# RMS statistics summed in pairs, a halved last block, and pooled output slots in a two-layer convolution trunk on eight cores

## Chip, cores, metric

The kernel is one program for all eight cores of one Trainium2 chip. Each core takes one prompt of 2048 tokens and 16 of the 128 short sequences of 4 tokens, so every core has the same work on its own data: 2112 tokens, cut into four blocks of 512 and one of 64. The metric is device time in microseconds (us) of the slowest core.

The program has a second, slower state in some executions, whatever the kernel: the cores of a die show a lower granted clock (the share of its full clock that TensorE is given: 0.81 to 0.98 on the slow dies here, 0.98 to 0.99 elsewhere) and the time is 3 to 19 per cent longer.

## Reference, cut to what matters

```python
def rmsnorm(x, g):
    xf = x.astype(jnp.float32)
    xn = xf * lax.rsqrt(jnp.mean(xf * xf, axis=-1, keepdims=True) + RMS_EPS)
    return xn.astype(x.dtype) * g

def hybrid_layer(x, ...):                       # D_MODEL 1024, DEPTH 2
    h = rmsnorm(x, norm_g)
    p = h @ w_in                                # 7 * 1024 columns: a_val, a_gate, z_a, gb, gc, hb, z_b
    u = a_val * sigmoid(a_gate)
    y_a = silu(head_layernorm(causal_dwconv(u, width 31))) * silu(z_a)
    y_b = gb * causal_dwconv(gc * hb, width 3) * silu(z_b)
    return x + concat(y_a, y_b) @ w_out         # and the last convolution rows
# two layers, then rmsnorm(x, final_g)
```

So there are three norms: one ahead of layer 0 (at the start, while x is still being loaded), one between the layers ("the border"), and one at the end.

## The kernel before: the parts that matter

The kernel is not written in program order. Each operation is entered into a scheduler with the tiles it reads and writes and a modelled duration; a simulation of the engines in Python then fixes one static order for each engine and queue.

x is held feature-major (128 features by tokens, eight tiles `k`). A norm needs the sum of squares over features, that is over partitions, which a matmul with a constant 1/1024 matrix (`ones_s`) gives. ScalarE squares two tiles at once; TensorE takes one matmul for each tile, eight for a block:

```python
def rms_stat(q, fill=None):                       # q: token block
    b = V("bank", "stat")
    for kp in range(4):
        s = V("tmp")
        act(... Square of x tiles 2*kp and 2*kp+1 -> tmph[:, s.slot, 0:2*n] ...)
        mm("stat", b, n, [(ones_s, tmph[:, s.slot, i*n:(i+1)*n]) for i in range(2)], ...)
    # ScalarE: Ln, then Exp(-0.5 *) -> r

def rms_apply(gcol0, q, r, final=False):          # eight VectorE multiplies x * g * r
    ...                                           # final: the result goes out, two tiles a DMA

def out_final(l, chunks, yslots, order, gcol0, final):    # last output projection of a layer
    for q in order:                               # last layer: blocks [0, 1, 4, 2, 3]
        for m in range(KC):
            out_block(q, m, lhs, ws + tps, yslots)        # 8 matmuls, VectorE adds the bank to x
        r = rms_stat(q)
        rms_apply(gcol0, q, r, final)
```

The gate outputs y of a layer need eight full-width slots at the end, and there are only five. The other three are borrowed from `u_sb` (two) and `up_sb`, the convolution's buffers. A borrowed slot has the resource of the *whole* buffer, so a reader of block 0 waits for the writer of block 4:

```python
def y_res(slot, q):
    if slot < NY:        return [y_r[slot][q]]    # own slot: one resource for each block
    if slot < NY + 2:    return u_r[slot - NY]    # borrowed: all blocks
    return [up_r, uph_r]
```

The convolution of head group A goes by way of DRAM, all on the queue of the SP engine, in order: `scr_u <- u_sb` (768 KB), `up_sb <- scr_u` (regrouped), convolution and LayerNorm in tile `big`, `scr_c <- big` (640 KB), `big <- scr_c` (640 KB, "the conv row"). The projection z_A of the same head is entered with the conv row as an explicit dependency, although the matmul doesn't read it (a ScalarE operation does, whose result is multiplied with z_A later):

```python
    o = spdma(... big[:, cn.slot] <- scr_c[l, j] ...)
    cn_of[(l, j, "op")] = o
def ln_z(l, j, slot):
    ...
    bz = proj(w, q, after=[cn_of[(l, j, "op")]], name=f"z{j}.{q}")
```

## Time and profile before

| before | us |
|---|---|
| time, median of 3 runs | 1146.0 (1145.72, 1146.0, 1204.93) |
| spans of the eight cores in the profiled run | 1138.2 to 1143.9 |

First the page of the slowest core (core 4): span, busy time with share and number of instructions, and the head of the chain of waits, which follows the work that ended last back to what released it.

```profile
span 1143.9 us, 20833 instructions; the slowest of 8 cores (1138.2 to 1143.9 us)
...
PE 1111.0 (97%) x7118; PEld 547.9 (48%) x7118; DVE 758.1 (66%) x1547; ACT 431.9 (38%) x680; POOL 187.7 (16%) x336
...
PE 92%; DMA 4%; DVE 2%; issue 1%; ACT 1%; SPq 0%; DVEq 0%; POOL 0%; ACTq 0%; POOLq 0%
```

TensorE (PE) is busy 97% of the span and is 92% of the chain: the time can only fall if TensorE gets less work or fewer gaps. The list of TensorE's waits on the same core (what it waited for: us in all, times, the longest; `psb` is the matmul's output, `wsl` and `toep` hold weights, L550 is a line of the kernel) has few gaps:

```profile
PE psb L550 <- ACT tmp L571: 6.0, 8, 1.6
PE psb L550 <- DVE h_sb L590: 5.5, 2, 2.9
PE psb L550 <- DMA wsl<-w_in_r: 5.2, 4, 1.9
PE psb L550 <- DVE up_sb L791: 4.5, 2, 2.2
PE psb L844 <- DVE ones_s L848: 1.5, 1, 1.5
```

The first two are the norms of the start and the end (squares, then h). The fourth is the borrowed slot. In the timeline (start, duration, engine, line, operation, count, in brackets the idle time before and what ended it) it stands at the head of layer 0's last output projection:

```profile
516.16 1.86 PE L550 MATMUL psb<-y_sb,wsl 128*128 128x512 bf16 x4 [2.24 <-DVE up_sb L791]
517.82 0.63 PE L550 MATMUL psb<-y_sb,toep 128*128 128x512 bf16 x1
...
519.46 1.03 PE L550 MATMUL psb<-y_sb,wsl 128*128 128x512 bf16 x4
```

After the wait eight matmuls take 3.30 us, 0.41 us each on average (0.427 us from start to start in the middle of the stretch); then they start every 0.215 us. The granted clock was 0.52 in this stretch (516.16 to 519.50), and 1.00 from 57 to 514. So a wait can cost more than its own length.

The end, on the same core (rows of other engines and weight loads left out). The last output matmul starts at 1129.09 and the next matmul at 1129.30; then the squares, the ones-matmuls, Ln and Exp, eight multiplies and the output follow one another:

```profile
1129.30 1.03 PE L550 MATMUL psb<-tmp,ones_s 128*128 128x512 bf16 x4
1129.38 2.47 DVE L800 TENSOR_TENSOR x_sb<-x_sb,psb 128x512 f32<-128x512 f32 x4
...
1133.15 0.59 PE L550 MATMUL psb<-tmp,ones_s 128*128 128x512 bf16 x2 [0.60 <-ACT tmp L571]
...
1134.53 0.63 ACT L581 ACTIVATE tmp<-tmp 128x512 f32<-128x512 f32 x1
1135.26 5.39 DVE L590 SCALAR_TENSOR_TENSOR x_sb<-x_sb,vecs_sb,tmp 128x512 f32<-128x512 f32 x8 [3.40 <-ACT tmp L581]
```

### The profile page before, as it was taken

What the parts mean: (1) busy time and instruction counts of PE and PEld (TensorE: products, weight loads), DVE (VectorE), ACT (ScalarE), POOL (GpSimd) and SP (SyncE); (2) the same over time, 40 slices, a digit from 0 to 9 for tenths busy, and PEclk for the clock granted to TensorE, in tenths of its full rate; (3) what the DMA queues carried; (4) which work ended last, traced back from release to release, by engine and by line L of the source; (5) the groups of instructions that cost most, each with busy time, mean ns of one, the idle gap of its engine ahead of it and who ended that gap; (6) DMA issues with size and microseconds to landing.
All of it is one profiled execution on the core that took longest, in us unless ns stands there. A gap on an engine that the chain in (4) does not pass through costs nothing.

```text
span 1143.9 us, 20833 instructions; the slowest of 8 cores (1138.2 to 1143.9 us)
## 1 busy us (share of the span) xinstructions
PE 1111.0 (97%) x7118; PEld 547.9 (48%) x7118; DVE 758.1 (66%) x1547; ACT 431.9 (38%) x680; POOL 187.7 (16%) x336
## 2 busy tenths in 40 slices
PE   6899999999999999999999999999999999999995
PEld 4345454455445455444444455445544545544442
DVE  2674866986876587653674486598688566774475
ACT  3751443343413444533342143433451253454232
POOL 1421222022102021000032122111120202110000
PEclk8999999999999999999999999999999999999998
DMA  8837667466726466731021757656761745563043
GB/s 192 230 82 144 101 133 136 84 107 118 129 35 111 84 119 111 127 67 19 1 43 30 144 114 141 139 87 113 126 98 42 142 87 104 92 81 105 1 157 147
DMA packets 177286, 117.97 MB, mean 103 GB/s; under 512 B 139104, under 2 KB 150240, under 8 KB 177120
## 3 DMA queue, kind: packets, MB, share of 16 engines
q0 software_dynamic: 32544, 48.41, 28.9%
q1 hardware_dynamic: 144496, 68.21, 23.9%
q8 instruction: 59, 0.97, 0.3%
q14 instruction: 43, 0.35, 0.1%
q10 hardware_dynamic: 144, 0.03, 0.0%
HBM read 132.24 MB, written 36.19 MB: 147 GB/s over the span
## 4 chain that ended last, share of the span: by engine, by line
PE 92%; DMA 4%; DVE 2%; issue 1%; ACT 1%; SPq 0%; DVEq 0%; POOL 0%; ACTq 0%; POOLq 0%
PE psb L550 88%; DMA wsl<-w_in_r 2%; PE psb L666 2%; DMA x_sb<-x_d 2%; PE psb L668 2%; DVE x_sb L590 1%; DVE h_sb L590 0%; SPq L834 0%; DVE x_sb L800 0%; ACT tmp L571 0%; ACT tmp L581 0%; ACT tmp L579 0%; DVE up_sb L791 0%; ACT L579 0%; DVE tmp L789 0%
## 5 line engine op out<-in xcount | busy, mean ns | idle before, releaser
L550 PE MATMUL psb<-h_sb,wsl 128*128 128x512 bf16 (+1 forms) x4480 | 821.8, 343 | 10.8 <-DVE h_sb L590 5.5
L550 PEld LDWEIGHTS psb<-h_sb,wsl 128*128 128x128 bf16 x4480 | 373.2, 98 | 417.1 <-issue 16.6
L550 PE MATMUL psb<-y_sb,wsl 128*128 128x512 bf16 (+1 forms) x960 | 186.6, 343 | 4.5 <-DVE up_sb L791 4.5
L800 DVE TENSOR_TENSOR x_sb<-x_sb,psb 128x512 f32<-128x512 f32 (+1 forms) x240 | 133.8, 591 | 63.3 <-PE psb L550 62.6
L541 POOL DMA_DIRECT2D wsl<-w_in_r x112 | 60.3, 545 | 432.5 <-PE psb L550 321.4
L550 PEld LDWEIGHTS psb<-y_sb,wsl 128*128 128x128 bf16 x960 | 82.3, 98 | 94.6 <-issue 5.7
L782 DVE SCALAR_TENSOR_TENSOR tmp<-vbuf,cw_b_sb,tmp 128x512 f32<-128x512 bf16 (+1 forms) x160 | 102.8, 660 | 21.9 <-POOL vbuf L764 11.6
L607 DVE SCALAR_TENSOR_TENSOR u_sb<-tmp,psb 128x512 bf16<-128x512 f32 (+1 forms) x80 | 47.3, 592 | 98.6 <-PE psb L550 88.3
L605 ACT ACTIVATE tmp<-psb 128x512 f32<-128x512 f32 (+1 forms) x80 | 41.1, 521 | 144.5 <-PE psb L550 139.6
L752 DVE TENSOR_TENSOR vbuf<-psb,tmp 128x512 bf16<-128x512 f32 (+1 forms) x80 | 47.3, 594 | 63.8 <-PE psb L550 61.3
L644 DVE COPY toep<-wt_sb 32x512 bf16<-32x512 bf16 x256 | 77.4, 304 | 12.7 <-DMA wt_sb<-wt_d 0.9
L571 ACT ACTIVATE tmp<-x_sb 128x1024 bf16<-128x1024 f32 (+1 forms) x60 | 52.6, 901 | 82.7 <-DVE x_sb L800 75.3
L741 ACT ACTIVATE tmp<-psb 128x512 f32<-128x512 f32 (+1 forms) x80 | 40.6, 521 | 103.8 <-PE psb L550 92.6
L787 ACT ACTIVATE tmp<-psb 128x512 f32<-128x512 f32 (+1 forms) x80 | 41.2, 521 | 96.3 <-PE psb L550 89.9
L779 ACT ACTIVATE tmp<-vbuf,cw_b_sb 128x512 f32<-128x512 bf16 (+1 forms) x80 | 50.9, 642 | 57.0 <-DVE vbuf L752 51.6
L673 DVE TENSOR_TENSOR big<-psb,cbt_sb 128x320 bf16<-128x320 f32 x128 | 62.1, 485 | 14.6 <-PE psb L668 10.6
L750 ACT ACTIVATE tmp<-psb 128x512 f32<-128x512 f32 (+1 forms) x80 | 41.0, 519 | 73.1 <-PE psb L550 71.7
L736 ACT ACTIVATE tmp<-big,vecs_sb 128x512 f32<-128x512 bf16 (+1 forms) x80 | 55.1, 730 | 33.2 <-DMA big<-scr_c 32.3
L590 DVE SCALAR_TENSOR_TENSOR h_sb<-x_sb,vecs_sb,tmp 128x512 bf16<-128x512 f32 (+1 forms) x80 | 47.1, 657 | 30.0 <-ACT tmp L581 30.0
L789 DVE TENSOR_TENSOR tmp<-psb,tmp 128x512 f32<-128x512 f32 (+1 forms) x80 | 46.8, 594 | 26.4 <-PE psb L550 25.2
L638 POOL DMA_DIRECT2D wt_sb<-wt_d x64 | 34.4, 538 | 171.3 <-DVE toep L644 125.0
L666 PE MATMUL psb<-up_sb,toep 128*128 128x96 bf16 x512 | 49.0, 207 | 0.0
(64 smaller groups left out, 794.1 us busy)
## 6 DMA issues: line engine op xcount, KB each, us to landing
wsl<-w_in_r POOLq DMA_DIRECT2D x112, 256.0 KB, 6.0
scr_u<-u_sb SPq DMA_DIRECT2D x16, 768.0 KB, 6.5
up_sb<-scr_u SPq DMA_DIRECT2D x16, 768.0 KB, 8.4
scr_c<-big SPq DMA_DIRECT2D x16, 640.0 KB, 6.3
big<-scr_c SPq DMA_DIRECT2D x16, 640.0 KB, 5.5
x_sb<-x_d SPq DMA_DIRECT2D x16, 512.0 KB, 12.0
wt_sb<-wt_d POOLq DMA_DIRECT2D x64, 128.0 KB, 4.3
y_fm<-x_sb SPq DMA_DIRECT2D x16, 512.0 KB, 2.7
```

Source lines behind the costliest of these rows:

```text
L541: return e.dma_start(out=wsl[:, v.slot, :], in_=src)
L550: ins = e.matmul(bank(v, n), lhsT=l_(), rhs=r_(), start=(first and i == 0), stop=(last and i == len(pairs) - 1))
L571: act((lambda e, s=s, kp=kp: e.activation(out=tmph[:, s.slot, 0:2 * n], in_=x_sb[:, KC * c0 + 2 * kp * n:KC * c0 + (2 * kp + 2) * n], func ...
L590: dve((lambda e, k=k, out=out: e.scalar_tensor_tensor(out=out, in0=xv(k, q), scalar=vecs[:, gcol0 + k:gcol0 + k + 1], in1=tm(r, n), op0=AL ...
L607: dve((lambda e: e.scalar_tensor_tensor(out=u_blk(ub, q), in0=b3(tm(th, n), q), scalar=1.0, in1=b3(bank(bv, n), q), op0=ALU.add, op1=ALU.m ...
L644: dve((lambda e, p=p, c=c: e.tensor_copy(toep[p, tp.slot, :].rearrange("p (m x) -> p m x", x=128)[:, :, 32 * c:32 * c + 32], wt_sb[p, w.sl ...
L666: e.matmul(o, lhsT=toep[:, tp.slot, (m + 1) * 128:(m + 2) * 128], rhs=up_sb[:, g, :].rearrange("p (i c) -> p i c", i=2)[:, :, 0:48], start ...
L673: dve((lambda e, b=b, v=v, bias=bias: e.tensor_tensor(out=big[:, co.slot, 4 * b:4 * b + 4, :], in0=banks[v.slot][:, 0:384].rearrange("p (g ...
L736: act((lambda e, s=s, q=q, n=n: e.activation(out=b3(tm(s, n), q), in_=c_blk(cn.slot, q), func=AF.Silu, scale=vecs[:, 16 + col:17 + col], b ...
L779: act((lambda e, a=a, q=q, n=n: e.activation(out=b3(tm(a, n), q), in_=v_blk(q, 0), func=AF.Copy, scale=cw_b[:, l, j, 2:3])), n, [v_r[q], c ...
L782: dve((lambda e, a=a, q=q, n=n, lag=lag: e.scalar_tensor_tensor(out=b3(tm(a, n), q), in0=v_blk(q, lag), scalar=cw_b[:, l, j, 2 - lag:3 - l ...
L800: dve((lambda e: e.tensor_tensor(out=xv(m, q), in0=xv(m, q), in1=bank(v, n), op=ALU.add)), n, [v, x_r[m][q]], [x_r[m][q]], name=f"x{q}.{m}")
```

## The change

Four intentions, in one diff:

1. **Pairs.** The two squared tiles are added first (on GpSimd in the output projections, on VectorE at the start and for the last part), so four ones-matmuls do for eight. They are marked urgent: the scheduler need leave no slack between operand and matmul.
2. **Last block in halves**, 256 tokens each, and for halves three of the eight multiplies go to ScalarE and GpSimd. In the same loop, a block's multiplies are now entered after the next block's statistics (the deferral).
3. **Gate-output slots as a pool** with a resource for each block, borrowed slots too.
4. **Start**: the first weights wait for the first x chunk, not the second, and x block 1 for the first weight, not the second. The scheduler's DMA model is retuned (`DPRE`, `DLAT`), and the order of a layer's parts is written as a string with the same parts in the same order.

```diff
-DLAT = {"pool": 3.0, "sp": 1.8, "act": 1.6}
+DPRE = {"pool": 2.4, "sp": 1.5, "act": 1.5}
+DLAT = {"pool": 1.6, "sp": 0.9, "act": 0.9}
 ...
-                if e == "pe" and t > QUIET and any(... slack of operands ...):
+                if e == "pe" and t > QUIET and not o.urgent and any(... slack of operands ...):
 ...
-    def rms_stat(q, fill=None):
+    def rms_stat(part, fill=None, pool=False):
 ...
-            mm("stat", b, n, [(ones_s, tmph[:, s.slot, i * n:(i + 1) * n]) for i in range(2)],
-               [s, ones_r], first=kp == 0, last=kp == 3, name=f"ss{q}.{kp}")
+            S.op("pool" if pool else "dve", (... tmph[0:n] = tmph[0:n] + tmph[n:2 * n] ...), ...)
+            mm("stat", b, n, [(ones_s, tmph[:, s.slot, 0:n])],
+               [s, ones_r], first=kp == 0, last=kp == 3, urgent=True, name=f"ss{q}.{kp}")
 ...
-    def y_res(slot, q):               # borrowed: the whole buffer
-        ...
+    class Y:                          # every slot: self.res = rs(NB); borrowed: also after
+        ...                           # the buffer's earlier readers and writers
 ...
-        for q in order:
+        before = None
+        for part in order:
             for m in range(KC):
-                out_block(q, m, lhs, ws + tps, yslots)
-            r = rms_stat(q)
-            rms_apply(gcol0, q, r, final)
+                out_block(part, m, lhs, ws + tps, ys)
+            r = rms_stat(part, pool=part is not order[-1])
+            if before:
+                rms_apply(gcol0, *before, final, shared)
+            shared = (2, 5, 7) if part[2] == 256 else ()
+            before = part, r
+        rms_apply(gcol0, *before, final, shared)
 ...
-        g = [x_ops[1]] if l == 0 else []
+        g = [x_ops[0]] if l == 0 else []
-                x_load(q, after=[wA[1].load])
+                x_load(q, after=[wA[0].load])
 ...
-    [0, 1, 4, 2, 3] if last else [0, 1, 2, 3, 4]
+    [whole(4), whole(0), whole(1), whole(2), (3, 0, 256), (3, 256, 256)] if last else [whole(q) for q in range(NB)]
```

## The prediction

> **What bounds it now.** TensorE. The page has PE busy 1111.0 of 1143.9 us (97%), and PE is 92% of the chain of waits. The windows put 455.7 us of matmul in the 457 us from 57 to 514, so mid-layer code has nothing to give. PE's other idle time: about 12.4 us in the first 38.4 us (load-bound, DMA share 0.90), 2.24 us twice at the head of each last out projection (waiting for DVE's write of up_sb), 1.2 and 1.9 us for weights at 183 and 734, and 12.4 us in the last 13.9 us.
>
> **What changes.** The list of mid-layer work is the same; I expect nothing there.
>
> 1. Ones-matmuls: 120 become 64. In the timeline back-to-back 128x512 matmuls start every 0.215 us; a 512-token norm loses four, 0.86 us. Of twelve, one or two sit in the load-bound start and the last in the tail, so nine count: -8 us, and -0.3 for the 64-token ones.
> 2. 36 pair-adds go to POOL, which has 1 us of work in the 67 at 514-581. No such op is in the trace[...]. The ones-matmul is now "urgent", placed with no slack, so a late add stalls PE: +2.5 us. DVE in an out-projection block does 8 x 0.684 + 8 x 0.75 = 11.5 us of about 14.6[...].
> 3. Gate outputs as per-block resources: block 0 of the last out projection no longer waits for all of up_sb. -4.3 us of wait, and -1.7 in layer 0, where the matmuls after the wait started every 0.41 us for eight of them (granted clock 0.97 there).
> 4. Tail. Now: last out matmul near 1129.3, end 1143.9: 14.6 us (add 0.69, square 1.06, ones, Ln 0.60, Exp 0.63, eight multiplies 5.4, output 3.2). With a 256-token half DVE first finishes six 512 multiplies of block 2, so the last add lands 1.5 us after PE; then square 0.6, pair-add, ones, Ln and Exp 0.9, five multiplies 2.1 with ACT and POOL doing three, output 3.2: about 9.4 us. -5.2 us.
> 5. Start: weights issue after the first x chunk (6.9 instead of 8.6 us), x block 1 after the first weight. Still bandwidth-bound: -1.5 us.
> 6. Small waits at the layer border (0.46 us) and the changed DMA model: -0.5.
>
> Sum: -8.3 - 6.0 - 5.2 - 1.5 - 0.5 + 2.5 = -19 us, all on the PE chain or its ends. Predicted **1127 us** (-1.7%), 8 in 10 between 1119 and 1135. Chances: faster by over 2% 0.22, within 2% 0.77, slower 0.01.
>
> **What shows each step.** (1) About half as many matmuls reading tmp and ones_s; PE busy near 1101. (2) PE's wait for POOL tmp 1 to 4 us[...]. (3) PE's wait for DVE up_sb gone. (4) Last out matmul to the end 9 to 10 us. (5) First h matmul near 15 us.
>
> **What would make it wrong.** POOL adds of 2 us[...], so that each stalls PE (36 x 0.3 = 11 us): 1135 or more. A start shorter by 5 us, or the weight waits gone too: under 1122. New weight waits from reshuffled slots: +3. A mid-layer gain would mean I missed a bound.

## More of the kernel before

One more view, which I did not look at closely before predicting. It is the SP queue on core 1 around the first convolution. The conv row of head 0 is asked for as soon as its source has been written, and `scr_u` comes later (at 158.99):

```profile
133.25 0.37 SPq L707 DMA_DIRECT2D scr_c<-big  x1
139.58 0.33 SPq L710 DMA_DIRECT2D big<-scr_c  x1
153.59 0.36 SPq L629 DMA_DIRECT2D up_sb<-scr_u  x1
```

No core of the kernel before has a TensorE wait for `big<-scr_c`.

## The result, and the profile after

| | median, us | fast runs, us |
|---|---|---|
| changed | 1134.03 | 1133.09, 1133.85, 1134.2 |
| before, same rounds | 1175.47 | 1145.72, 1146.0 |

Each kernel had four executions; one of the changed kernel (1251.41) and two of the one before (1204.93 and 1280.25) fell in the slow state, which is why the median of before means little here. **The ratio is 0.9894 (95%: 0.9865 to 0.9923).** Ratios are computed everywhere as the mean time of one kernel's fast runs over that of the other's of the same rounds, so they are not quite the ratio of the quoted medians. The gain is 12 us; in a repeat of five rounds (below) it was 14. I had predicted 19, and 1127.

The page of the changed kernel's slowest core, core 1, with the group of pair-adds:

```profile
span 1131.7 us, 21055 instructions; the slowest of 8 cores (1122.8 to 1131.7 us)
...
PE 1101.1 (97%) x7126; PEld 549.1 (49%) x7126; DVE 777.8 (69%) x1585; ACT 439.2 (39%) x694; POOL 231.8 (20%) x378
...
PE 91%; DMA 4%; DVE 2%; ACT 1%; issue 1%; POOL 0%; SPq 0%; DVEq 0%; ACTq 0%; POOLq 0%
...
L603 POOL TENSOR_TENSOR tmp<-tmp 128x512 bf16<-128x512 bf16 (+2 forms) x36 | 39.1, 1091 | 96.6 <-ACT tmp L601 96.6
```

TensorE's busy time fell by the 10 us I had named. The spread of the cores grew from 5.7 to 8.9 us: the median core gained 14.1 us (1141.1 to 1127.0), the slowest only 12.2. TensorE's waits on core 1:

```profile
PE psb L556 <- DVE tmp L603: 8.6, 8, 2.1
PE psb L556 <- DVE h_sb L629: 5.2, 2, 2.6
PE psb L556 <- DMA big<-scr_c: 2.8, 1, 2.8
...
PE psb L556 <- DMA wsl<-w_in_r: 1.4, 2, 0.7
PE psb L556 <- POOL tmp L603: 1.2, 2, 1.0
PE psb L556 <- ACT tmp L801: 0.9, 1, 0.9
```

The wait for `up_sb` is gone, GpSimd's adds are waited for only 1.2 us, and there is a **new wait for `big<-scr_c`, one of 2.8 us**. The changed kernel's head of the last output projection, on this core, follows the projection before it without a gap, and matmuls are 0.215 us apart from the first on:

```profile
511.76 5.38 PE L556 MATMUL psb<-h_sb,wsl 128*128 128x512 bf16 x38
516.98 1.03 PE L556 MATMUL psb<-y_sb,wsl 128*128 128x512 bf16 x4
```

The new wait, in the timeline of core 1 (SP queue and TensorE rows):

```profile
143.28 0.37 SPq L747 DMA_DIRECT2D scr_c<-big  x1
150.39 0.33 SPq L662 DMA_DIRECT2D scr_u<-u_sb  x1
...
151.29 1.37 SPq L750 DMA_DIRECT2D big<-scr_c  x1
...
162.46 5.02 PE L556 MATMUL psb<-h_sb,wsl 128*128 128x512 bf16 x16 [2.83 <-DMA big<-scr_c]
```

Here `scr_u`, 768 KB, is issued ahead of the conv row, where before it came behind it. The row is asked for at 151.29 and lets TensorE go at 162.46, 11 us later; the page gives 4.9 us from issue to landing as the median of the sixteen such loads, and the same load of head 0 took 6.6 us on this core before. The wait is on no core before; after, it is on six of eight cores, once each, from 0.2 to 2.8 us in this run.

**The wait costs more than its own 2.8 us.** The sixteen matmuls after it take 5.02 us, 0.31 us each, because the first seven start 0.38 to 0.43 us apart again (granted clock 0.50 from 162.46 to 165.20; after core 7's wait it was 1.00). Only cores 1 and 4 (waits of 2.83 and 2.12 us) have such a stretch of half-speed matmuls there, and they are the two slowest cores of this run: from the first convolution to the first output projection they take 96.4 and 96.2 us, core 7, which waits 2.31 us without them, 94.5, and core 6, which doesn't wait, 92.0.

The end (last output matmul at 1121.08, weight loads and other rows left out):

```profile
1121.46 0.42 DVE L852 TENSOR_TENSOR x_sb<-x_sb,psb 128x256 f32<-128x256 f32 x1 [0.30 <-PE psb L556]
...
1123.10 5.05 DVE L629 SCALAR_TENSOR_TENSOR x_sb<-x_sb,vecs_sb,tmp 128x256 f32<-128x256 f32 x9
1123.23 0.27 PE L556 MATMUL psb<-tmp,ones_s 128*128 128x256 bf16 x1 [0.33 <-DVE tmp L603]
...
1124.07 0.42 ACT L613 ACTIVATE tmp<-tmp 128x256 f32<-128x256 f32 x1
1124.63 2.44 POOL L626 TENSOR_TENSOR x_sb<-x_sb,tmp 128x256 f32<-128x256 f32 x3 [3.82 <-ACT tmp L613]
```

From the start of the last output matmul to the start of the last Exp it is 3.0 us here; it was 5.4 before (1129.09 to 1134.53).

**Where the time went, by stage.** I cut every core's trace at landmarks on TensorE (first matmul on h of a layer, first convolution matmul, first output projection, first matmul on `u_sb` in the last output projection, last output matmul) and took the median of the eight cores, in us. The first and the third row are sums of the medians of shorter stages (cut at the first matmul on h and, in the first row, at the first convolution too); the median of the whole first stage is 201.2 before and 200.9 after. The last matmul's landmark is its recorded end:

| stage | before | after | difference | predicted |
|---|---|---|---|---|
| start to first output projection of layer 0 | 200.73 | 200.69 | 0.0 | -3.2 |
| output projection to last one, layer 0 | 314.51 | 312.26 | -2.3 | -2.15 |
| last projection of layer 0 to first conv of layer 1 (border) | 137.28 | 134.13 | -3.2 | -4.6 |
| first conv to first output projection, layer 1 | 95.67 | 96.40 | +0.7 | 0 |
| output projection to last one, layer 1 | 314.30 | 312.15 | -2.2 | -2.15 |
| last projection to the last output matmul | 62.55 | 60.69 | -1.9 | |
| last output matmul to end | 14.64 | 10.35 | -4.3 | -6.7 with the line above |
| sum | 1139.68 | 1126.67 | -13.0 | -18.8 |

The predicted column puts the terms of the prediction where they belong: -3.2 is the -1.5 for the gates and two norms at 0.86; -4.6 is four and a bit norms (-3.6), the half-speed matmuls (-1.7), the small waits (-0.5) and half of the adds' cost (+1.2); -6.7 is -5.2, three norms (-2.7) and the other half (+1.2). The biggest miss is the first row. Another landmark splits it: the time at which the median core has passed its first 240 times 512 columns through useful matmuls (ones-matmuls not counted) fell from 82.0 to 80.3 us. So the start did gain, and **nearly all of it was lost again before the first output projection**.

### The profile page after: what moved, and what is told of

Read it like the earlier page. It is cut to its first block, busy times and chain, and to the rows that moved or that the text cites. A ratio compares the mean times of both kernels' runs of the same rounds, so it can differ in the third digit from the quotient of the medians.

```text
span 1131.7 us, 21055 instructions; the slowest of 8 cores (1122.8 to 1131.7 us)
## 1 busy us (share of the span) xinstructions
PE 1101.1 (97%) x7126; PEld 549.1 (49%) x7126; DVE 777.8 (69%) x1585; ACT 439.2 (39%) x694; POOL 231.8 (20%) x378
## 4 chain that ended last, share of the span: by engine, by line
PE 91%; DMA 4%; DVE 2%; ACT 1%; issue 1%; POOL 0%; SPq 0%; DVEq 0%; ACTq 0%; POOLq 0%
PE psb L556 88%; DMA x_sb<-x_d 2%; PE psb L706 2%; PE psb L708 1%; DMA wsl<-w_in_r 1%; DMA big<-scr_c 1%; DVE x_sb L629 1%; DVE x_sb L852 1%; DVE h_sb L629 0%; POOL tmp L603 0%; ACT big L738 0%; ACT tmp L601 0%; ACT tmp L613 0%; SPq L891 0%; ACT tmp L611 0%
## 5 line engine op out<-in xcount | busy, mean ns | idle before, releaser
L556 PE MATMUL psb<-y_sb,wsl 128*128 128x512 bf16 (+2 forms) x992 | 188.1, 336 | 0.8 <-DVE x_sb L852 0.7
L852 DVE TENSOR_TENSOR x_sb<-x_sb,psb 128x512 f32<-128x512 f32 (+2 forms) x248 | 136.2, 575 | 42.0 <-PE psb L556 41.0
L556 PEld LDWEIGHTS psb<-y_sb,wsl 128*128 128x128 bf16 x992 | 85.2, 98 | 87.6 <-issue 1.6
L601 ACT ACTIVATE tmp<-x_sb 128x1024 bf16<-128x1024 f32 (+2 forms) x64 | 53.9, 859 | 87.0 <-DVE x_sb L852 70.9
L629 DVE SCALAR_TENSOR_TENSOR h_sb<-x_sb,vecs_sb,tmp 128x512 bf16<-128x512 f32 (+1 forms) x80 | 52.6, 711 | 11.8 <-ACT tmp L613 11.7
L603 POOL TENSOR_TENSOR tmp<-tmp 128x512 bf16<-128x512 bf16 (+2 forms) x36 | 39.1, 1091 | 96.6 <-ACT tmp L601 96.6
```

The source lines that it names most:

```text
L556: ins = e.matmul(bank(v, n), lhsT=l_(), rhs=r_(), start=(first and i == 0), stop=(last and i == len(pairs) - 1))
L601: act((lambda e, s=s, kp=kp: e.activation(out=tmph[:, s.slot, 0:2 * n].rearrange("p (k c) -> p k c", k=2), in_=x2(kp, part), func=AF.Square)),
L629: dve((lambda e, k=k, out=out: e.scalar_tensor_tensor(out=out, in0=xs(k, part), scalar=vecs[:, gcol0 + k:gcol0 + k + 1], in1=tm(r, n), op0 ...
L852: dve((lambda e: e.tensor_tensor(out=xs(m, part), in0=xs(m, part), in1=bank(v, n), op=ALU.add)), n, [v, xr], [xr], name=f"x{q}.{m}")
```

## The experiments

All runs had five rounds against the kernel before, which had medians of 1146.5 to 1147.8 us (of its fast runs alone, 1146.3 to 1147.7). Those of one prefix (c1, c2, c3, c4) ran on the same chip in the same rounds. An interval is about 0.002 to each side, or 2 us; so where 1 to 3 us are at stake I use the stage times as well, where most stages repeat within a few tenths. "Same order" means that the edit is made after scheduling, or hidden from the scheduler, so that every engine keeps the changed kernel's order; the lists are identical, and the traces show the same order of instructions.

### 1. The change again, and its matmuls, adds and gates (same order)

**c1_after**: no edit.

> The changed kernel again, on this chip, as the control for the three runs below. Expected 1133 to 1135 us, 0.988 to 0.991 of the kernel before. A theory is not tested here; it tells whether the gain of 12 us holds on another chip and gives the stage times that the frozen-order variants are held against.

Measured: 1133.06 us, ratio 0.9876 (0.9858 to 0.9894). The stages repeat. The wait for `big<-scr_c` falls on other cores this time, up to 3.2 us (cores 0, 1, 2, 3, 4 and 6).

**c1_twice**: each ones-matmul issued twice, with half the constant.

```diff
-    dve(lambda e: e.memset(ones_s[:], 1.0 / D), ...)
+    dve(lambda e: e.memset(ones_s[:], 0.5 / D), ...)
-            mm("stat", b, n, [(ones_s, tmph[:, s.slot, 0:n])], ...)
+            mm("stat", b, n, [(ones_s, tmph[:, s.slot, 0:n])] * 2, ..., cost=1)   # modelled as one
```

> Changed kernel with the order of every engine frozen; each ones-matmul is issued twice at half weight (the result stays right), so TensorE gets the removed matmuls back while the pair-adds stay. Theory A (the matmuls saved in the load-bound start are worth nothing, the others their full 0.215 us): the 44 of 512, 8 of 256 and 12 of 64 tokens cost 10.7 us if all count; the 8 of blocks 0 and 1 are hidden, so +8.5 us (7.5 to 9.5) over the control, with the time at which 60 units of useful work are done moved by under 0.7 us. Rival B (the ones-matmuls now wait for their adds, so the adds and not the matmul count decide): under +5 us. Rival C (every matmul counts, the start's too): +10.7 us, and 60 units later by 1.7 us.

Measured: 1139.11 us, ratio 0.9929 (0.9914 to 0.9944), 6.0 us over c1_after. By stage 1.4 us at the start (240 units), 3.0 at the border, 2.6 in the last projection: 7.0. So halving them saved 6 to 7 us, where I had counted 8.3; that lies between theory A (7.5 to 9.5) and rival B (under 5).

**c1_tinyadd**: the pair-add takes 2 columns, not n. Its output is wrong, which doesn't matter for the time. Everything else stays.

```diff
-                out=tmph[:, s.slot, 0:n], in0=tmph[:, s.slot, 0:n], in1=tmph[:, s.slot, n:2 * n], op=ALU.add
+                out=tmph[:, s.slot, 0:2], in0=tmph[:, s.slot, 0:2], in1=tmph[:, s.slot, n:n + 2], op=ALU.add
```

> Changed kernel, frozen order, each pair-add shortened to 2 columns (wrong result on purpose): takes away the adds' time on POOL and DVE and what they hold back, keeps every wait and every instruction. Theory A (adds cost little: PE waits about 1.2 us for POOL, the start's chain carries one 0.42 us add per block): -1.5 to -3 us. Rival B (late adds[...] ate the missing 7 us): -5 us or more.

Measured: fast runs 1129.56 to 1134.02 us (median 1131.6; one more run was slow), ratio 0.9858 (0.9838 to 0.9878). By stage it takes 1.4 us off the border and 1.2 off the last projection, 2.6 in all, near the predicted +2.5; the whole time shows 1.4 us by the medians and 2.1 by the ratios, with an error of about 2. The short adds are still in the program and still waited for, so this is a lower bound. Still, slow GpSimd adds are not where 6 us went.

**c1_gate**: the two gates of the start put back.

```diff
     S.run()
+    # first two weights wait for x_ops[1] again, x block 1 for the second weight
+    for o in gate_w: o.deps.discard(x_ops[0]); o.deps.add(x_ops[1])
+    for o in x_ops[4:]: o.deps.discard(gate_x[0]); o.deps.add(gate_x[1])
```

> Changed kernel, frozen order, the start's load gates put back (first weights after the second x chunk, x block 1 after the second weight). Theory A (the start is bound by bytes; the earlier gates bring x block 1 a little sooner but slow x block 0): +1.2 us (0.3 to 2), first useful matmul about 0.5 us earlier, 60 units of useful work 1 to 1.5 us later. Rival D (the new gates do harm because weights compete with x block 0): -1 us or better.

Measured: 1135.79 us, ratio 0.9902 (0.9885 to 0.9918): 2.7 us by the medians, 2.3 at the 240-unit mark (82.4 against 80.1), more than theory A's 0.3 to 2; the first matmul on h did not move (16.7 us in both). The gate matters, but see c3_nopair: without pairs it gives nothing.

What follows: the terms for matmuls, adds and gates are near their predicted sizes or about 1 us smaller; none holds the missing 5 to 7 us. The new wait was the next suspect.

### 2. The new wait, the slots, and the end

**c2_nowait** (same order): the z_A matmuls no longer wait for the conv row. They don't read it, so this is free of races; ScalarE's reader of the row still waits.

```diff
     S.run()
+    for o in S.ops:
+        if o.eng == "pe" and o.name.startswith("z") and not o.name.startswith("zb"):
+            o.deps -= {conv-row loads}
```

> Changed kernel, frozen order; the eight z_A projections of each layer no longer wait on TensorE for the load of the normalised conv rows (big from scr_c), which they do not read; ScalarE, which reads it, still waits. Theory E (the reshuffled order puts the first of these projections of layer 0 ahead of its load: a DMA-dependent wait of 0 to 6 us by core, which the slowest core pays): first conv to first out projection within 1.5 us over the cores instead of 3 to 6, every core near 92.5 us there, and 1.5 to 3 us off the time, so 1130 to 1131.5. Rival F (ScalarE waits for the same load anyway and TensorE only stalls one step later, at its banks): under 0.7 us.

Measured: 1129.7 us (1129.07 to 1130.61), ratio 0.9848 (0.983 to 0.9867), correct. The stage from first conv to first output projection of layer 0 falls from 93.7 (c1_after, cores 92.2 to 95.4) to 92.4 us, **and all cores lie between 92.0 and 92.9**. The stage sum to the first output projection is 198.9, against 200.7 before, so the 1.8 us of the start are kept.

**c2_slots**: the kernel before, with per-block resources for the borrowed slots only.

```diff
 def y_res(slot, q):
     if slot < NY:
         return [y_r[slot][q]]
-    if slot < NY + 2:
-        return u_r[slot - NY]
-    return [up_r, uph_r]
+    return [latey(slot)[0][q]]        # rs(NB) for each borrowed slot; the writer also waits
+                                      # for the buffer's earlier readers and writers
```

> Kernel before, with one part of the change: the borrowed gate-output places (u_sb, up_sb) become resources per block. TensorE's order is the same as before. Theory L (this is the whole worth of the slot part: the 2.24 us wait twice, 1.6 us of half-rate matmuls after it in layer 0): -4.5 to -6 us against before, the wait for DVE up_sb gone, first to last out projection stage shorter by 2.2 to 3.5 us in each layer. Rival M (another operand, the weights or other banks, is ready only just then): -1.5 us or less.

Measured: fast runs 1138.24 to 1140.93 us (median 1139.4; two more runs were slow), ratio 0.9933 (0.9913 to 0.9953): 7.1 us under before by the medians of fast runs, 7.6 by the ratio. By stage -2.5 in each layer ahead of the last projection, -0.35 at the border, and -0.76 and -0.23 in the last two stages, 6.3 in all. The predicted -6.0 is right by the stages and somewhat low by the run times. The run covers the borrowed slots alone; the pool for the other five was not run by itself.

**c2_noshare**: halves, but all multiplies on VectorE.

```diff
-            shared = (2, 5, 7) if part[2] == 256 else ()
+            shared = ()
```

> Changed kernel, but all 16 multiplies of the two halves stay on DVE (no ScalarE scale, no POOL multiply); the order of TensorE is the same. Theory G (sharing takes six half multiplies of 0.45 us off DVE, [...] it gives about half of that): last out matmul to end 10.35 becomes 11.5 to 12.7 us, total +1.2 to +2.4. Rival H [...]: within 0.4 us of the changed kernel. Rival I (sharing pays in full): +2.7 or more.

Measured: 1134.37 us, ratio 0.988 (0.9861 to 0.9899). Last output matmul to end: 10.72 instead of 10.35 us. Sharing over three engines is worth 0.4 us. The half in theory G was my estimate; what keeps sharing from paying in full was not shown.

**c2_alldve**: all pair-adds on VectorE.

```diff
-            r = rms_stat(part, pool=part is not order[-1])
+            r = rms_stat(part)
```

> Changed kernel with all pair-adds on DVE (0.42 us each[...]) instead of 36 on POOL (1.1 us); the order is scheduled anew. The shortened adds took 1.4 us off the layer border and 1.2 off the final projection. Theory J (that was [...] late POOL adds; DVE has room for 4 x 0.42 us per block): both stages shorten by 0.8 to 1.4 us, total -1 to -2.5 against the changed kernel, if the mid-layer order is not hurt. Rival K (DVE is too full there): both stages the same or longer.

Measured: fast runs 1131.87 to 1134.92 us, ratio 0.9884 (0.986 to 0.9908); three more runs were slow. The last projection gains 1.2 us and the border 0.6, and the end loses 1.55: no gain. VectorE's add takes 0.42 us against GpSimd's 1.25, but in the end stage, where this loses 1.55 us, VectorE has more to do; that this is the reason was not tested.

The wait for `big<-scr_c` thus carried about 3 us of the slowest core. But why did it appear? The compiled kernels' instruction lists, not run, gave a lead: the kernel before plus pairs alone (a build that was never run) has `scr_u` ahead of the conv row, and the changed kernel without pairs (c3_nopair below) has it behind.

### 3. Queue order, and the rest of the end

**c3_queue** (same order but for this): the conv row of head 0 put back two places in the SP queue, ahead of `scr_u` and a small output.

```diff
     S.run()
+    q = S.order["sp"]; i = q.index(cn_of[(0, 0, "op")])
+    q.insert(i - 2, q.pop(i))         # and the positions renumbered
```

> Changed kernel, frozen order but for one thing: on the SP queue the first load of normalised conv rows (big from scr_c) of layer 0 goes ahead of the 768 KB write of u_sb to scr_u and a small output, as in the kernel before; in the changed kernel it stands behind both. TensorE still waits for that load. Theory N (that queue order is what makes the load late): the wait for big from scr_c is gone or under 0.7 us on every core, first conv to first out projection 92 to 93 us on every core, total 2.5 to 3.5 us under the changed kernel (about 1130), as the run without TensorE's wait. Rival O (the place of the projection on TensorE is too early whatever the queue does): waits of 1 us or more stay, total within 1 us. Risk: the written rows come later and the next conv waits for up_sb.

Measured: 1130.66 us (1130.02 to 1131.23), ratio 0.9862 (0.9847 to 0.9878). The SP queue on core 1:

```profile
139.67 0.37 SPq L747 DMA_DIRECT2D scr_c<-big  x1
146.69 0.33 SPq L750 DMA_DIRECT2D big<-scr_c  x1
147.18 0.33 SPq L662 DMA_DIRECT2D scr_u<-u_sb  x1
```

The wait is left on two cores, at most 0.9 us at a time; the stage is 92.3 us (92.0 to 93.1), as in c2_nowait. So the place of this load on the queue made most of the wait. From issue to landing it takes 7.0 us here (median of the eight cores; 6.0 to 9.9), against 9.7 (7.5 to 11.0) in the changed kernel and 6.3 (5.4 to 6.8) in the one before. What is left fits the write `scr_c<-big` itself, which is later than before (133.25 us on core 1); no run separates that.

**c3_nopair**: the change without pair-adds (two ones-matmuls, no add, not urgent).

```diff
-            S.op("pool" if pool else "dve", (... add ...), ...)
-            mm("stat", b, n, [(ones_s, tmph[:, s.slot, 0:n])], [s, ones_r], ..., urgent=True)
+            mm("stat", b, n, [(ones_s, tmph[:, s.slot, i * n:(i + 1) * n]) for i in range(2)], [s, ones_r], ...)
```

> Changed kernel without the pair-adds: two ones-matmuls per square as before, not urgent, all else kept (scheduled anew; the SP queue then has the conv-row load ahead of the write again). Theory P (pairing is worth about 1.5 us in the start, 2.8 at the layer border, 1.1 in the final projection, and costs up to 3.4 on the slowest core through the moved load): +1.5 to +3.5 us against the changed kernel by the run times, layer border (first out projection of the last round to first conv of layer 1) 136.5 to 137.2 us, final projection 61.5 to 62.0, fastest core 1127 to 1130. Rival Q (the pairing pays its full 8 us less nothing): +6 us or more.

Measured: fast runs 1134.89 to 1136.57 us, ratio 0.9909 (0.9894 to 0.9925), so pairs as a whole gain about 3 us here. No core waits for the conv row, as the instruction lists had said, but every core has a weight wait of 1.6 to 2.5 us instead (2.3 on the slowest, at 184 us; before, these were 0.5 to 1.9), so this is not a clean measure of pairs. The 240-unit mark is 82.5: the new gates alone give nothing, and neither did pairs alone in c1_gate (82.4); both together give 2 us. Why they only act together I did not settle.

**c3_whole**: the last block not cut in halves.

```diff
-        [whole(4), whole(0), whole(1), whole(2), (3, 0, 256), (3, 256, 256)]
+        [whole(4), whole(0), whole(1), whole(2), whole(3)]
```

> Changed kernel with the last 512-token block whole and its norm on DVE alone (no halves, no sharing). Theory R (halving alone makes the tail short, as the run without sharing lost only 0.4 us): last out matmul to end 13.5 to 14.5 us instead of 10.35, total +3 to +4.2 us. Rival S (pair-add and earlier statistics shorten the whole-block tail too): tail under 12.5, total +2 or less.

Measured: fast runs 1132.37 to 1136.22 us, ratio 0.9894 (0.9875 to 0.9912). Last projection and end together: 72.11 us, against 71.04 for the change. **Halves and sharing together are worth 1.1 us**, where I had put 5.2 on them, so another part of the change shortens the end. (The stage after the last output matmul alone is 13.2 us, which fits neither theory; the stage before it is 1.8 us shorter than in the change.) VectorE's timeline shows which. In c2_slots (the loop of before) eight multiplies of the block before run in one piece, and the adds of the last block wait behind them:

```profile
1118.69 5.39 DVE L590 SCALAR_TENSOR_TENSOR x_sb<-x_sb,vecs_sb,tmp 128x512 f32<-128x512 f32 x8 [1.15 <-ACT tmp L581]
1124.00 2.47 DVE L809 TENSOR_TENSOR x_sb<-x_sb,psb 128x512 f32<-128x512 f32 x4
```

In c3_whole, with the same 512-token block, they alternate, so each add comes soon after its matmuls:

```profile
1117.37 0.74 DVE L629 SCALAR_TENSOR_TENSOR x_sb<-x_sb,vecs_sb,tmp 128x512 f32<-128x512 f32 x1
1118.16 0.69 DVE L852 TENSOR_TENSOR x_sb<-x_sb,psb 128x512 f32<-128x512 f32 x1
1118.76 1.41 DVE L629 SCALAR_TENSOR_TENSOR x_sb<-x_sb,vecs_sb,tmp 128x512 f32<-128x512 f32 x2
1120.09 0.68 DVE L852 TENSOR_TENSOR x_sb<-x_sb,psb 128x512 f32<-128x512 f32 x1
```

That is the deferral, two lines of the diff for which I had no term.

**c3_best**: c2_nowait, with the border's pair-adds on VectorE and the last projection's on GpSimd.

```diff
+    # z_A matmuls don't wait for the conv row (as c2_nowait)
-            r = rms_stat(part, pool=part is not order[-1])
+            r = rms_stat(part, pool=final and part is not order[-1])
```

> A version meant to beat both: the changed kernel, z_A projections no longer waiting on TensorE for the conv rows, pair-adds of the layer border on DVE and those of the final projection left on POOL. From the parts: 1129.7 of the run without the wait, less 0.6 us at the border (60.68 + 73.45 became 60.29 + 73.24 with all adds on DVE): 1129 (1128 to 1131). If DVE were too full at the border, that stage would be 60.7 us or more.

Measured: 1130.85 us, ratio 0.9865 (0.9849 to 0.9881). The border gains 0.6 us against c2_nowait (60.29+73.24 against 60.73+73.46 us), and the whole time shows nothing of it.

### 4. The deferral alone, and whether queue and wait are one cause

**c4_defer**: c2_slots with the deferral; **c4_nodefer**: the change without it.

```diff
             r = rms_stat(q)
-            rms_apply(gcol0, q, r, final)
+            if before:
+                rms_apply(gcol0, *before, final)
+            before = q, r
+        rms_apply(gcol0, *before, final)
```

> Kernel before, with the per-block borrowed places and one more part: a block's norm multiplies are emitted after the next block's adds and statistics (the change does this too; the prediction did not cost it). No pairs, no halves. Theory T (this ordering, not the halves, is most of the shorter end: DVE no longer does eight multiplies in a row, 5.4 us, ahead of the adds that the last statistics need): last projection plus tail 76.2 us of the run with per-block places alone becomes 72.5 to 74, time 2.2 to 3.7 us under it, about 1137.5. Rival U (only halving or pairing shortens the end): 75.7 us or more, time within 1 us.

> Changed kernel with that ordering undone (a block's multiplies right after its own statistics, as before), halves, sharing and pairs kept. Theory T: last projection plus tail 71.0 us becomes 72.5 to 74.5, total +1.5 to +3.5 us. Rival U: 71.5 or less, total within 0.7 us. (The conv-row wait stays, so the slowest core is noisy by 1 us; read the stage.)

Measured: c4_defer, fast runs 1135.49 to 1137.48 us, ratio 0.9904 (0.9889 to 0.9919); c4_nodefer, fast runs 1135.85 to 1139.35, ratio 0.9917 (0.9904 to 0.993). Last projection and end together, median core:

| kernel | us |
|---|---|
| c2_slots (slots alone) | 76.20 |
| c4_defer (slots, deferral) | 74.69 |
| c4_nodefer (change without deferral) | 74.29 |
| c3_nopair (change without pairs) | 72.67 |
| c3_whole (change without halves and sharing) | 72.11 |
| the change | 71.04 |

Taken out of the change, deferral costs 3.25 us, as theory T had it; pairs cost 1.6, halves and sharing 1.1. Put on c2_slots, deferral alone gives 1.5, which lies between T and U. The parts do not add up to a sum of single effects, but the deferral is the largest of those taken out. The change also puts the block of 64 tokens first in the last projection; no run separates that.

**c4_both**: c2_nowait and c3_queue together.

> Changed kernel, frozen order, with both mends: the conv-row load ahead of the write on the SP queue, and no wait for it on TensorE. Each alone gave 1130.7 and 1129.7 us. If the load was the one cause, the two do not add: 1129 to 1130.5. If a second cause was hidden behind it, under 1128.5.

Measured: fast runs 1129.56 to 1130.94 us, ratio 0.9849 (0.9836 to 0.9862). The stage is 92.1 us (92.0 to 92.6), 0.2 to 0.3 under either alone; the two take away the same loss.

The best version is c2_nowait, at 1129.7 us or 0.9848, and c3_queue and c4_both are equal to it within the error. All three beat the kernel before clearly; their fast runs also lie under the changed kernel's, but for one of c3_queue (1131.23, against 1131.21 for the fastest of c1_after), and that comparison is between chips.

## Why the prediction was right or wrong

**What bounds it: right.** TensorE's busy time fell from 1111.0 to 1101.1 us (I had said near 1101), and the gain is of that size.

**The step that failed: "The list of mid-layer work is the same; I expect nothing there."** The list is the same; its order is not. I read the list where the machine follows an order, and the order comes from a scheduler that the change feeds with new durations and new operations. The pairs moved `scr_u` ahead of the conv row on the SP queue (without them, in c3_nopair, it is behind again); TensorE then waited for that row at the first z_A projection of layer 0, up to 2.8 us in the profiled run and 3.2 in the repeat, on different cores in the two runs. Since the time is that of the slowest core, the largest wait counts, and with it the half-speed matmuls that can follow (0.427 us apart on cores 1 and 4): on core 1 of the profiled run this stage was 4.4 us longer than on core 6, which didn't wait. Removing the dependency (c2_nowait) gave 3.4 us by the medians, 3.2 by ratios; putting the load back (c3_queue) 2.4 and 1.6; both together no more. This is the largest single loss, 2 to 3 of the missing 5 to 7 us. My list of risks had "new weight waits from reshuffled slots: +3": the size fits, but it was another load on another queue, and I did not put it into the sum. Weight waits came as well, but smaller (see 6). The dependency was there before and cost nothing as long as the row came early.

Point by point, with the other terms:

- **(1) Ones-matmuls, -8.3.** Mis-sized by a little: 6.0 us in the whole time, 7.0 by stages (c1_twice).
- **(2) Adds on GpSimd, +2.5.** Right in size: 2.6 us by stages (c1_tinyadd), at the least. The +2.5 was an estimate: no trace had shown such an add then. In the changed kernel's trace (core 1) an add of 512 columns takes 1.15 us where no VectorE multiply runs beside it (at 1070.61), and 1.25 as the mean of the 28. Beside multiplies both can take longer. Two VectorE multiplies take 1.41 us together (in c3_whole above), and 2.36 or 2.30 with a GpSimd add within them; of the two adds below the first takes 1.15 us, the second 1.64, and the longest on this core 1.71. Why they take longer was not tested:

```profile
1085.75 2.36 DVE L629 SCALAR_TENSOR_TENSOR x_sb<-x_sb,vecs_sb,tmp 128x512 f32<-128x512 f32 x2
...
1089.90 2.30 DVE L629 SCALAR_TENSOR_TENSOR x_sb<-x_sb,vecs_sb,tmp 128x512 f32<-128x512 f32 x2
```

```profile
1085.75 1.15 POOL L603 TENSOR_TENSOR tmp<-tmp 128x512 bf16<-128x512 bf16 x1 [3.08 <-ACT tmp L601]
1090.01 1.64 POOL L603 TENSOR_TENSOR tmp<-tmp 128x512 bf16<-128x512 bf16 x1 [3.10 <-ACT tmp L601]
```

Most of it hides behind TensorE, as expected: TensorE waits for a GpSimd add 1.2 us in the whole run.
- **(3) Slots, -6.0.** Right: 6.3 us by stages, 7.1 to 7.6 by run times (c2_slots). The 1.7 us for half-speed matmuls in layer 0 were read from core 4 alone. The other cores' traces of before have such half-speed matmuls after the same wait on cores 0, 1 and 2 and none on 3, 5, 6 and 7; in layer 1, where I had counted none, they are on cores 2, 3, 5 and 6. Cores 4, 2 and 1 were the slowest three, so the term counted, but reading its size from one core was luck.
- **(4) Tail, -5.2.** The size was near, the reason wrong. The stage from last output matmul to end fell by 4.3 us. But halves and sharing, to which I gave it all, are worth 1.1 us, and sharing alone 0.4; the deferral is worth 3.25 within the change. I had computed the new end as if the order of VectorE's work were fixed by the halves, so the near size is luck.
- **(5) Start, -1.5.** With the first norms' matmuls I expected -3.2 there; it was 1.7 to 2 (82.0 to 80.3 or 80.1 us at the 240-unit mark). Gates and pairs act only together. The first matmul on h, which I expected near 15 us, did not come sooner: 16.3 us before, 16.9 after (medians).
- **(6) Small, -0.5.** Not found. Every core has a new wait of 0.9 to 1.1 us on ScalarE, in the middle of layer 0 (at 287 to 295 us), which I did not follow up. The stage from the first conv to the first output projection of layer 1 is 0.4 to 1.3 us longer in every kernel made from the changed one, and not in c2_slots and c4_defer. The traces show weight waits there (`wsl<-w_in_r`, near 725 us): 0.2 to 1.7 us on seven of eight cores after, 0.2 to 1.9 on four before, and 95.5 to 95.7 us for the stage on the cores without one. No run takes them away.

By stages, on the median core, the 5.8 us between -18.8 and -13.0 are, but for rounding: 1.8 for the conv row (200.69 to 198.91 us with c2_nowait), 1.4 at the start, 2.0 in the border and the last two stages together (predicted -11.3, measured -9.3), 0.7 in layer 1. On the slowest core the conv row is the larger part.

About why the row lands late the runs show this much: behind a 768 KB write on the same queue, issued 0.9 us before it, this load lands 9.7 us after its issue, and on every core after the write (by 1.7 to 5.3 us); when it goes first it takes 7.0 us (c3_queue; medians of the eight cores). What holds it up behind the write was not shown.

## What to carry to other kernels

Where a static scheduler fixes the order, compare the *order* of the two builds on every engine and queue, DMA queues above all, before saying that a stage is untouched: an equal list of operations says nothing about which load is asked for first. Give a matmul only dependencies on what it reads; an extra one costs nothing until something moves, and then what counts is the wait of the slowest core (here 2 to 3 us). And when a loop is rewritten, cost the moved line as well as the new operations: here the place of one call was worth more at the end than splitting a block over three engines.

## Hardware behaviour measured here

- Half-speed matmuls after a wait: a gap of 2.24 us was enough on core 4 of the kernel before (matmuls 0.427 us apart after it, granted clock 0.52), and one of 2.12 us on core 4 of the changed one (0.427 us, 0.53). With gaps of 2.24 to 2.32 us in layer 0 of the kernel before, the half rate came on four of eight cores and not on the others, and after a gap of 2.31 us on core 7 of the changed kernel it did not come (0.215 us, 1.00). So the length of the gap alone does not decide it; what does was not shown.
- GpSimd adds beside VectorE's multiplies: an add of two bf16 128x512 operands takes 1.15 us alone and 1.15 to 1.71 beside multiplies, and a pair of those 2.30 to 2.36 instead of 1.41 us.
- A load behind a large write on one queue: a 640 KB load behind a 768 KB write lands 9.7 us after its issue, and 7.0 us after it when it goes ahead of the write (medians of the eight cores).
- A dependency that an operation doesn't need cost 2 to 3 us of the slowest core: the wait falls on other cores in other runs, and its largest value counts (cores 92.2 to 95.4 us in that stage with it, 92.0 to 92.9 without).
